# Moving 99 subtractions from GpSimd to VectorE in a hybrid Hyena and latent-attention layer

## The chip, the core and the metric

The kernel runs on one core of a Trainium2 chip, in one launch. The metric is the device time of one execution in microseconds (us). Five engines have queues of their own: TensorE (PE in the profile; PEld are its weight loads), VectorE (DVE), ScalarE (ACT), GpSimd (POOL) and SyncE (SP, which here only issues DMAs). An engine works its queue off in order; semaphores tie the queues to each other.

## The reference

```python
h = rms_norm(x, g_norm)                                   # x: (1, 1024, 1024) float32
proj = h @ w_in                                           # (1024, 1024) @ (1024, 5280)
hy_in, z_hy, c_q, c_kv, k_rope, z_attn, gate_hy, gate_attn = split(proj)
v_h, x1, x2 = split(short_conv(hy_in, w_short, b_short), 3)
k_spec = hyena_filter_spectra(...)                        # small MLP, two directions, rfft
zc = v_h
for o, gate in enumerate((x1, x2)):
    zc = gate * long_conv(zc, k_spec[:, o], hy_bias[o])   # FFT convolution, length 2048
u_hy = (zc * silu(z_hy)) @ w_hy_out
q, k, v = up-projections of rms_norm(c_q), rms_norm(c_kv); k_rope shared; rms_norm, rotary
u_attn = (attention(q, k, v) * silu(z_attn)) @ w_attn_out # 8 heads, 1024 x 1024 scores each
x + (sigmoid(gate_hy + b) * u_hy + sigmoid(gate_attn + b) * u_attn) @ w_out
```

Everything is float32.

## The kernel before

Every float32 product is made of three faster TensorE products: both operands are split into a high part (a cast on ScalarE, L133) and a low part (the operand less its high part, L134, a two-input subtraction), and high times high, low times high and high times low are summed in PSUM. `split` (L132) does that; its argument `eng` picks the engine of the subtraction, VectorE where none is given.

The stages follow one another on TensorE as follows. From 0 to 50 us `build_hT` loads and transposes x and makes `hh` and `hl`, the parts of the normalised input. From 50 to 250 us the filter's small MLP (`filter_mlp`, two sine layers of many VectorE steps), its tables and `filter_spectra` run: for each of 2 orders and 2 halves of the channels it forms, in four steps `tp`, the filter `kk` in both directions (PSUM times decay, L335), the sum `A` (L338, VectorE) and the difference `B` (L339, GpSimd). A butterfly on VectorE (`forward`) turns A and B into eight leaves, each split and multiplied with a table on TensorE (`leaf_fwd`, L128). From 250 to 650 us the four long convolutions (`conv`, `convs`) do the same forward and, leaf by leaf, back. From 650 to 775 us `qkv` and the rest of the projection follow, then attention, and from about 1020 us the tail with the output projections.

The big input projection is cut into 41 blocks of 128 columns and one of 32. `proj_block` (L538 on) makes one: for each of two halves of the rows it loads 128x512 weights `wr` (SP queue, 2 buffers), casts them to `wh` (ScalarE, 3 buffers), subtracts to `wl` (L134, on GpSimd, 3 buffers), and runs 24 products of 512 columns, among them `hh` times `wh`, `hl` times `wh` and `hh` times `wl` (L552). A half has to be consumed before its buffers take another. The last, small block (`proj_rope`, L565) does it in one piece. `branch_out` has a split of its own; its three calls with `mb == 1` are on GpSimd too, with the same tile names.

The queues do not have the order of the source: a planner places the instructions when the program is built, by durations of its own, and it may move any of them ahead of others that the data allow. Blocks of the projection are so mixed into the filter stage and the convolutions.

Of the kernel before, what the change touches and what calls it, by code (L numbers as in the profile page):

```python
# [10 lines left out]
F32 = mybir.dt.float32  # L11
# [3 lines left out]
ALU = mybir.AluOpType  # L15
# [77 lines left out]
class K:  # L93
# [219 lines left out]
    def filter_spectra(self, wk):  # L313
        nc, a = self.nc, self.a
        h2, w3h, w3l = self.h2, self.w3h, self.w3l
        kuh, kul = self.kuh, self.kul
        self.kd = {}
        for o in range(2):
            for hf in range(NHALF):
                A = wk.tile([P, 8, CW], F32, tag="A", name=self.nm("A"))  # L320
                B = wk.tile([P, 8, CW], F32, tag="B", name=self.nm("B"))
                cs = slice(hf * CW, (hf + 1) * CW)
                bia = wk.tile([1, CW], F32, tag="bia", bufs=2, name=self.nm("bia"))
                nc.sync.dma_start(out=bia, in_=a["hy_bias"][:, o, cs])
                for tp in range(4):
                    dec = wk.tile([P, 2, 2, CW], F32, tag="dec", bufs=2, name=self.nm("dec"))
                    nc.sync.dma_start(out=dec, in_=a["dec"][hf, tp].rearrange("p (d t c) -> p d t c", d=2, t=2))
                    kk = wk.tile([P, 2, 2, CW], F32, tag="kk", bufs=2, name=self.nm("kk"))
                    for d in range(2):
                        ps = self.pp.tile([P, 2, CW], F32, tag="cv", bufs=CVB, name=self.nm("pk"))  # L330
                        for i in range(2):
                            ts = slice((2 * tp + i) * P, (2 * tp + i + 1) * P)
                            nc.tensor.matmul(ps[:, i], lhsT=h2[d][:, ts], rhs=w3h[d][:, o, cs], start=True, stop=False)
                            nc.tensor.matmul(ps[:, i], lhsT=h2[d][:, ts], rhs=w3l[d][:, o, cs], start=False, stop=True)
                        nc.vector.tensor_tensor(out=kk[:, d], in0=ps, in1=dec[:, d], op=ALU.mult)  # L335
                    if tp == 0:
                        nc.vector.tensor_tensor(out=kk[0:1, 0, 0], in0=kk[0:1, 0, 0], in1=bia, op=ALU.add)
                    nc.vector.tensor_tensor(out=A[:, 2 * tp:2 * tp + 2], in0=kk[:, 0], in1=kk[:, 1], op=ALU.add)  # L338
                    nc.gpsimd.tensor_tensor(out=B[:, 2 * tp:2 * tp + 2], in0=kk[:, 0], in1=kk[:, 1], op=ALU.subtract)  # L339

                def take(k, ps):
                    if k == 0:
                        kt = wk.tile([P, 3, CW], F32, tag="kt0", bufs=1, name=self.nm("kt"))
                        nc.scalar.mul(out=kt[:, 0], in_=ps[:, 0], mul=2.0 ** -10)
                        nc.scalar.mul(out=kt[:, 1], in_=ps[:, 0], mul=2.0 ** -10)
                        nc.scalar.mul(out=kt[:, 2], in_=ps[:, 1], mul=2.0 ** -10)
                        nc.scalar.mul(out=kt[0:1, 1], in_=ps[0:1, 1], mul=2.0 ** -10)
                        nc.vector.memset(kt[0:1, 2], 0.0)
                        n = 3
                    else:  # L350
                        kt = wk.tile([P, 2, CW], F32, tag="kt", bufs=2, name=self.nm("kt"))
                        nc.scalar.mul(out=kt, in_=ps, mul=2.0 ** -10)
                        n = 2
                    kd = self.dp.tile([P, n, CW], F32, tag=f"kd{o}_{hf}_{k}", name=f"kd{o}_{hf}_{k + 8}")
                    nc.scalar.dma_start(out=kd, in_=kt)
                    self.kd[o, hf, k] = kd

                self.forward(A, B, kuh, kul, take)
# [178 lines left out]
    def proj_block(self, c0, m=P):  # L537

        nc, wp = self.nc, self.wp
        ps = [self.pp.tile([P, 512], F32, tag="mm", bufs=MMB, name=self.nm("pm")) for _ in range(2)]  # L540
        src = self.a["w_in"][0].rearrange("(d p) c -> p d c", p=P)
        for g in range(2):
            raw = wp.tile([P, 4, P], F32, tag="wr", bufs=2, name=self.nm("wr"))
            nc.sync.dma_start(out=raw[:, :, 0:m], in_=src[:, 4 * g:4 * g + 4, c0:c0 + m])
            wh = wp.tile([P, 4, P], F32R, tag="wh", bufs=3, name=self.nm("wh"))
            wl = wp.tile([P, 4, P], F32R, tag="wl", bufs=3, name=self.nm("wl"))
            self.split(raw[:, :, 0:m], wh[:, :, 0:m], wl[:, :, 0:m], self.nc.gpsimd)
            for i in range(4):
                d = 4 * g + i
                for (w, h, f) in ((wh, self.hh, 0), (wh, self.hl, 1), (wl, self.hh, 2)):  # L550
                    for c in range(2):
                        nc.tensor.matmul(ps[c][0:m], lhsT=w[:, i, 0:m], rhs=h[d][:, c * 512:(c + 1) * 512],  # L552
                                         start=(d == 0 and f == 0), stop=(d == 7 and f == 2))
        return ps

    def proj_rope(self, c0):

        nc, wp = self.nc, self.wp
        ps = [self.pp.tile([P, 512], F32, tag="mm", bufs=MMB, name=self.nm("pm")) for _ in range(2)]
        src = self.a["w_in"][0].rearrange("(d p) c -> p d c", p=P)  # L560
        raw = wp.tile([P, 8, 32], F32, tag="wr", bufs=2, name=self.nm("wr"))
        nc.sync.dma_start(out=raw, in_=src[:, :, c0:c0 + 32])
        w = wp.tile([P, 8, 64], F32R, tag="wh", bufs=3, name=self.nm("wh"))
        nc.scalar.copy(out=w[:, :, 0:32], in_=raw)
        nc.gpsimd.tensor_tensor(out=w[:, :, 32:64], in0=raw, in1=w[:, :, 0:32].bitcast(F32), op=ALU.subtract)  # L565
        for d in range(8):
            for f, h in enumerate((self.hh, self.hl)):
                for c in range(2):
                    nc.tensor.matmul(ps[c][0:64], lhsT=w[:, d], rhs=h[d][:, c * 512:(c + 1) * 512],
                                     start=(d == 0 and f == 0), stop=(d == 7 and f == 1))  # L570
        return ps
# [662 lines left out]
```

## Time and profile before

| | us |
|---|---|
| median of 3 runs (lowest, highest) | 1190.2 (1189.45, 1192.81) |
| the profiled execution | 1190.89 |
| its span, first to last instruction | 1189.1 |
| TensorE busy in the span | 1115.7 |
| VectorE busy | 899.3 |
| ScalarE busy | 584.0 |
| GpSimd busy | 282.9 |

Busy times are sums over the whole span; the stages have different limits, so the sections below go by stretches of it. TensorE's records overlap one another (a pair of products of 512 columns is recorded with 0.62 us around 736 us, and the next pair starts 0.45 us after it), so its idle time says more than its busy time. Of the 85 GpSimd subtractions called `wl`, 82 are the projection's and 3 those of `branch_out`.

### The profile page before, as it was taken

To read this page: it belongs to the slowest core of one execution; us is meant where nothing else is said; L and a number is where in the kernel's file an instruction comes from. 1 tells how busy PE (TensorE), PEld (TensorE's weight loads), DVE (VectorE), ACT (ScalarE), POOL (GpSimd) and SP (SyncE) were. 2 spreads that over 40 slices of the span, in tenths; PEclk is the share of its full clock that TensorE was granted. 3 is DMA by queue.
4 is the path that set the end of the run, shared out by engine and by line. 5 is a ranking of instruction groups with operands and counts; after the bars stand their busy time and mean duration, and the time that the engine had idled before them with its cause. 6 is when DMAs were issued, how large, how long until landed. Compare 5 with 4: busy or idle time off the path is not lost. (4 is left out here: it accounts for less than half of the span.)

```text
span 1189.1 us, 15596 instructions
## 1 busy us (share of the span) xinstructions
PE 1115.7 (94%) x5541; PEld 913.5 (77%) x5541; DVE 899.3 (76%) x1530; ACT 584.0 (49%) x1096; POOL 282.9 (24%) x217
## 2 busy tenths in 40 slices
PE   4989898999999999999999998999999999999996
PEld 3767777787888777787878887788887888777875
DVE  5889889977877986777764892188888898768873
ACT  5554455464424532434425742477777777422320
POOL 3333331333112121212111144500000000132253
PEclk7989999999999999999999999899999999999999
DMA  5334543553233424334227557620201010686245
GB/s 195 79 110 136 173 170 117 174 173 98 80 112 101 133 76 159 97 98 129 74 88 238 144 171 261 208 89 1 98 1 63 28 53 10 215 293 211 88 132 176
DMA packets 119221, 150.27 MB, mean 126 GB/s; under 512 B 8548, under 2 KB 82408, under 8 KB 119144
## 3 DMA queue, kind: packets, MB, share of 16 engines
q1 hardware_dynamic: 107832, 122.88, 33.6%
q10 hardware_dynamic: 11312, 26.42, 6.1%
q8 instruction: 43, 0.70, 0.3%
q14 instruction: 34, 0.28, 0.1%
HBM read 101.81 MB, written 47.45 MB: 126 GB/s over the span
## 5 line engine op out<-in xcount | busy, mean ns | idle before, releaser
L134 POOL TENSOR_TENSOR wl<-wr,wh 128x512 fp32r<-128x512 f32 x85 | 139.3, 1642 | 387.1 <-ACT wh L133 361.5
L552 PE MATMUL pm<-hh,wl 128*128 128x512 f32 x656 | 210.1, 396 | 3.2 <-POOL wl L134 3.2
L552 PE MATMUL pm<-hl,wh 128*128 128x512 f32 x656 | 212.5, 397 | 0.3 <-POOL hl L134 0.2
L552 PE MATMUL pm<-hh,wh 128*128 128x512 f32 x656 | 211.0, 397 | 1.7 <-ACT wh L133 1.7
L552 PEld LDWEIGHTS pm<-hh,wl 128*128 128x128 f32 x656 | 124.2, 190 | 29.6 <-POOL wl L134 4.1
L552 PEld LDWEIGHTS pm<-hh,wh 128*128 128x128 f32 x656 | 124.1, 190 | 28.1 <-ACT wh L133 2.5
L552 PEld LDWEIGHTS pm<-hl,wh 128*128 128x128 f32 x656 | 124.4, 190 | 27.0 <-DVE hl L134 1.0
L133 ACT CAST wh<-wr 128x512 fp32r<-128x512 f32 x98 | 60.3, 619 | 155.0 <-PE pm L552 108.4
L134 DVE TENSOR_TENSOR PTl<-pt,PTh 128x512 fp32r<-128x512 f32 x128 | 84.0, 683 | 14.0 <-ACT PTh L133 11.3
L133 ACT CAST PTh<-pt 128x512 fp32r<-128x512 f32 x128 | 72.8, 587 | 43.6 <-PE pt L886 41.0
L871 DVE TENSOR_REDUCE mx<-S 128x1 f32<-128x1024 f32 x64 | 77.8, 1218 | 10.5 <-PE S L122 10.0
L886 PE MATMUL pt<-ident,pr 128*128 128x128 f32 x512 | 75.1, 276 | 1.1 <-DVE PTl L134 0.5
L873 ACT ACTIVATE pr<-S,mx 128x1024 f32<-128x1024 f32 x64 | 71.7, 1120 | 5.4 <-DVE mx L871 5.1
L886 PEld LDWEIGHTS pt<-ident,pr 128*128 128x128 f32 x512 | 59.1, 140 | 15.5 <-ACT pr L873 2.9
L898 PE MATMUL pv<-PTh,vc 128*128 128x256 f32 x256 | 68.9, 297 | 0.0
L133 ACT CAST rh<-res 128x512 fp32r<-128x512 f32 x64 | 39.3, 617 | 59.3 <-DVE res L366 29.3
L899 PE MATMUL pv<-PTl,vc 128*128 128x256 f32 x256 | 67.8, 293 | 0.0
L458 DVE TENSOR_TENSOR t<-pu,kt 128x512 f32<-128x512 f32 x64 | 41.1, 682 | 34.8 <-PE pu L128 34.1
L967 DVE TENSOR_TENSOR gg<-gg,pmo 128x512 f32<-128x512 f32 x32 | 21.7, 679 | 46.9 <-DMA gT<-ob 44.1
L134 POOL TENSOR_TENSOR vc<-vr,vc 128x512 fp32r<-128x512 f32 x8 | 10.2, 1284 | 196.1 <-ACT vc L133 196.1
L118 PE MATMUL S<-kh,qh 96*128 96x512 f32 x128 | 53.0, 414 | 1.7 <-ACT pr L873 1.6
L121 PE MATMUL S<-kh,ql 96*128 96x512 f32 x128 | 52.5, 410 | 0.0
(289 smaller groups left out, 2580.8 us busy)
## 6 DMA issues: line engine op xcount, KB each, us to landing
wr<-in_w_in_dram SPq DMA_DIRECT2D x82, 256.0 KB, 3.0
wor<-in_w_out_dram SPq DMA_DIRECT2D x36, 256.0 KB, 5.1
dec<-in_dec_dram SPq DMA_DIRECT2D x16, 512.0 KB, 3.8
gT<-ob ACTq DMA_DIRECT2D x16, 512.0 KB, 3.6
gg<-gT SPq DMA_DIRECT2D x16, 512.0 KB, 4.7
kd<-kt ACTq DMA_DIRECT2D x28, 256.0 KB, 2.5
kt<-kd SPq DMA_DIRECT2D x28, 256.0 KB, 2.6
x<-in_x_dram SPq DMA_DIRECT2D x8, 512.0 KB, 6.2
```

The source lines that it names most:

```text
L118: m = nc.tensor.matmul(out, lhsT=lh, rhs=rh, start=start, stop=False)
L121: nc.tensor.matmul(out, lhsT=ll, rhs=rh, start=False, stop=False)
L133: self.nc.scalar.copy(out=hi, in_=x)
L134: (eng or self.nc.vector).tensor_tensor(out=lo, in0=x, in1=hi.bitcast(F32), op=ALU.subtract)
L458: tt = lambda o_, x, y, op: v.tensor_tensor(out=o_, in0=x, in1=y, op=op)
L552: nc.tensor.matmul(ps[c][0:m], lhsT=w[:, i, 0:m], rhs=h[d][:, c * 512:(c + 1) * 512], start=(d == 0 and f == 0), stop=(d == 7 and f == 2))
L871: nc.vector.tensor_reduce(out=mx, in_=ps, axis=AX.X, op=ALU.max, negate=True)
L873: nc.scalar.activation(out=pr, in_=ps, func=AF.Exp, bias=mx, accum_out=RS[h // 2][:, qb, h % 2:h % 2 + 1])
L886: nc.tensor.transpose(out=pt[:, i], in_=pr[:, kb * P:(kb + 1) * P], identity=self.ident)
L898: nc.tensor.matmul(pv, lhsT=V[h][:, kb], rhs=hi[:, kb], start=(kb == 0), stop=False)
L899: nc.tensor.matmul(pv, lhsT=V[h][:, kb], rhs=lo[:, kb], start=False, stop=(kb == 7))
L967: nc.vector.tensor_tensor(out=g[:, sl], in0=g[:, sl], in1=ps, op=ALU.mult)
```

## The change

Three subtractions go from GpSimd's queue to VectorE's: `B` in `filter_spectra` (16 instructions), the low part `wl` in `proj_block` (82) and the one in `proj_rope` (1). Operands, buffers, casts and DMAs are the same, and so is what is computed. GpSimd keeps its part in `build_hT` (`hl`, `zl`), in `qkv` (`k`), in `hyena_load` (`yl`), attention (`vc`), three splits of `branch_out` and the tail; between 50 and 650 us it is left with memsets alone.

```diff
@@ filter_spectra
                     nc.vector.tensor_tensor(out=A[:, 2 * tp:2 * tp + 2], in0=kk[:, 0], in1=kk[:, 1], op=ALU.add)
-                    nc.gpsimd.tensor_tensor(out=B[:, 2 * tp:2 * tp + 2], in0=kk[:, 0], in1=kk[:, 1], op=ALU.subtract)
+                    nc.vector.tensor_tensor(out=B[:, 2 * tp:2 * tp + 2], in0=kk[:, 0], in1=kk[:, 1], op=ALU.subtract)
@@ proj_block
-            self.split(raw[:, :, 0:m], wh[:, :, 0:m], wl[:, :, 0:m], self.nc.gpsimd)
+            self.split(raw[:, :, 0:m], wh[:, :, 0:m], wl[:, :, 0:m])
@@ proj_rope
-        nc.gpsimd.tensor_tensor(out=w[:, :, 32:64], in0=raw, in1=w[:, :, 0:32].bitcast(F32), op=ALU.subtract)
+        nc.vector.tensor_tensor(out=w[:, :, 32:64], in0=raw, in1=w[:, :, 0:32].bitcast(F32), op=ALU.subtract)
```

## Rows read from the trace of the kernel before

**Rows 1.** Busy time by stretch: us, then PE, PEld, DVE, ACT, POOL, clock, DMA, GB/s
```profile
50.00:250.00 200.00, 182.86 (x857) 146.78 (x856) 173.25 (x277) 107.25 (x206) 60.08 (x49) 0.97 0.46 147
250.00:650.00 400.00, 390.24 (x1781) 315.71 (x1780) 297.81 (x557) 167.41 (x329) 86.81 (x60) 1.00 0.39 116
650.00:775.00 125.00, 115.72 (x528) 95.85 (x526) 70.20 (x190) 60.81 (x113) 47.13 (x35) 0.97 0.61 192
```

**Rows 2.** Waits, 50 to 650 us: who waited for whom, us, times, longest
```profile
PE pu L128 <- ACT rh L133: 9.5, 7, 2.4
PE pm L552 <- POOL wl L134: 0.2, 1, 0.2
...
ACT wh L133 <- PE pm L552: 107.8, 28, 7.7
```

**Rows 3.** Durations by line and tile: minimum, median, maximum in ns
```profile
L134 DVE TENSOR_TENSOR rl<-res,rh x64: 669/679/1390, 104.7 to 593.0; 128x512 fp32r<-128x512 f32 x64
L335 DVE TENSOR_TENSOR kk<-pk,dec x32: 674/680/693, 86.1 to 218.5; 128x512 f32<-128x512 f32 x32
L338 DVE TENSOR_TENSOR A<-kk x16: 693/1477/1785, 88.2 to 219.4; 128x512 f32<-128x512 f32 x16
```

**Rows 4.** The group of projection subtractions on GpSimd, 50 to 250, then 250 to 650 us
```profile
L134 POOL TENSOR_TENSOR wl<-wr,wh 128x512 fp32r<-128x512 f32 x19 | 33.3, 1754 | 76.1 <-ACT wh L133 69.6 <-PE pu L128 5.8 <-PE pm L552 0.7
...
L134 POOL TENSOR_TENSOR wl<-wr,wh 128x512 fp32r<-128x512 f32 x51 | 85.1, 1670 | 302.3 <-ACT wh L133 288.0 <-PE pm L552 10.2 <-DMA wr<-in_w_in_dram 4.2
```

**Rows 5.** In order of time, one step of the filter: VectorE, then GpSimd
```profile
97.77 1.78 DVE L338 TENSOR_TENSOR A<-kk 128x512 f32<-128x512 f32 x1
...
97.60 1.41 POOL L339 TENSOR_TENSOR B<-kk 128x512 f32<-128x512 f32 x1 [1.83 <-DVE kk L335]
```

**Rows 6.** In order of time, VectorE: lengthened instructions beside GpSimd reads
```profile
62.70 1.07 DVE L245 SCALAR_TENSOR_TENSOR sx<-sk,sx 128x512 f32<-128x512 f32 x1
64.03 0.68 DVE L245 SCALAR_TENSOR_TENSOR sx<-sk,sx 128x512 f32<-128x512 f32 x1
67.17 1.78 DVE L245 SCALAR_TENSOR_TENSOR sx<-sk,sx 128x512 f32<-128x512 f32 x1
65.90 1.35 DVE L134 TENSOR_TENSOR kul<-kur,kuh 128x1152 fp32r<-128x1152 f32 x1
68.88 2.41 DVE L134 TENSOR_TENSOR kul<-kur,kuh 128x1152 fp32r<-128x1152 f32 x1
237.70 0.74 DVE L367 SCALAR_TENSOR_TENSOR res<-w,w 128x256 f32<-128x256 f32 x2
240.34 1.67 DVE L367 SCALAR_TENSOR_TENSOR res<-w,w 128x256 f32<-128x256 f32 x2
253.19 1.90 DVE L584 SCALAR_TENSOR_TENSOR acc<-sraw,cols,acc 128x1024 f32<-128x1024 f32 x1 [0.34 <-ACT acc L583]
642.56 1.21 DVE L138 SCALAR_TENSOR_TENSOR cl<-cr,cols,ch 128x256 fp32r<-128x256 f32 x1 [0.23 <-ACT ch L137]
```

**Rows 7.** In order of time around 740 us: TensorE, then GpSimd
```profile
739.94 0.73 PE L552 MATMUL pm<-hh,wh 128*128 128x512 f32 x2 [1.70 <-ACT wh L133]
744.13 1.22 PE L552 MATMUL pm<-hh,wl 128*128 128x512 f32 x2 [2.99 <-POOL wl L134]
738.17 4.68 POOL L134 TENSOR_TENSOR yl<-yr,yh 128x1024 fp32r<-128x1024 f32 x2 [9.97 <-ACT yh L133]
742.81 1.26 POOL L134 TENSOR_TENSOR wl<-wr,wh 128x512 fp32r<-128x512 f32 x1
```

**Rows 8.** Busy time by stretch as in rows 1, at two places
```profile
745.00:750.00 5.00, 5.00 (x13) 3.83 (x13) 0.00 (x0) 3.16 (x6) 5.00 (x4) 0.51 0.84 264
70.00:78.00 8.00, 5.94 (x19) 5.08 (x20) 7.74 (x8) 2.48 (x4) 2.00 (x4) 0.57 0.35 94
```

**Rows 9.** In order of time, TensorE: its waits in the filter stage
```profile
72.06 0.58 PE L333 MATMUL pk<-w3h,h 128*128 128x256 f32 x1 [3.69 <-DVE h L291]
104.56 0.41 PE L128 MATMUL pu<-rh,kuh 128*128 128x256 f32 x1 [2.36 <-ACT rh L133]
```

## The prediction

> **What bounds the kernel now.** I read the busy time by stretch first, then what TensorE waits for, then durations of the moved operations and of what runs beside them. TensorE is the bound: it is idle for 17.1 us between 50 and 250 us (200 less 182.9), for 9.8 us between 250 and 650 and for 9.3 us between 650 and 775 [rows 1]. Work taken off any other engine can only give back what lies in those 36 us, or what a low TensorE clock costs behind an idle time. VectorE is second: busy for 173.3 us of 200 in the filter stage, with 26.8 idle, and for 297.8 of 400 in the convolutions [rows 1]. TensorE's waits in these 600 us are for the ends of VectorE's chains (a cast of `res`, 9.5 us); for the moved `wl` it waits 0.2 us [rows 2]. So the change matters in two ways: by what it does to VectorE's chains, and by the one place after 650 us where `wl` was late.
>
> **What one moved instruction costs on VectorE.** The same operation, shape and type is there already: `rl<-res,rh`, 0.68 us in the median [rows 3]. I take 0.68 us for each of `wl` and `B`, and 0.4 us for the half-size one of `proj_rope` (an estimate by size).
>
> **What it gives back on VectorE.** An instruction there with both inputs in SBUF that meets a GpSimd subtraction waits for the rest of it. `A` and `B` are released together and read the same `kk`: `A` takes 1.48 us in the median and 0.69 when alone, while `kk<-pk,dec`, whose one input is in PSUM, never leaves 0.67 to 0.69 [rows 3]; one such meeting is shown, `B` from 97.60 and `A` for 1.78 us [rows 5]. I summed, over all VectorE instructions that overlap a GpSimd read which the change moves, their duration less that of the same shape alone. From 50 to 250 us that is 25.3 us in 28 instructions, the first of them the sine step at 62.70 (1.07 us for 0.68), the last within the pair at 240.34 (1.67 us, where the pair before took 0.74); from 250 to 650 us it is 26.6 us in 32 instructions, from 253.19 to 642.56 [rows 6].
>
> The Trainium skill (SBUF — State Buffer, section Who interferes with whom) has this as a rule: a VectorE instruction with two SBUF inputs and a GpSimd one that reads SBUF lock each other out, and whoever issues first keeps the port for its whole length. The trace agrees, with 1.48 us for `A` and 0.68 for `kk`.
>
> **50 to 250 us.** On VectorE come 19 `wl` [rows 4] and 16 `B`, as many as there are `A` [rows 3]: 35 times 0.68 is 23.8 us; 25.3 us go. The load falls by 1.5 us, in effect not at all. What can change is the length of the chains for which TensorE stands. In the MLP it waits 3.69 us for `h` at 72.06 [rows 9]; three stalls are in VectorE's queue ahead of it, 0.39 and 1.10 us in sine steps and 1.06 us in `kul` [rows 6], 2.55 us in all, and three `wl` (2.0 us) take their place if the planner leaves them there. That is -0.5 to -2.6 us, and the clock is granted at 0.57 from 70 to 78 us after that wait [rows 8], so a shorter wait may also save part of 3.4 us (8 times 0.43). In each of the four filter steps some 3.1 us of stalls on `A` go (4 times 0.78) against four `B` (2.7 us); about four `wl` come (2.7 us) against the quarter of what other stalls are left, 2.6 us (25.3 less 2.55 less 12.5, over 4). Net -0.3 us each, -1.2 for four, more if the planner sets `B`, which only the last four leaves need, behind the sums. TensorE's wait at 104.56, 2.36 us, shows that the end of such a step is bare [rows 9]. I take -3 us for this stage. The bounds are -17, all of its idle time, and +10, if the `wl` of the four steps stand bare (10.8 us, less the 1.2).
>
> **250 to 650 us.** 51 `wl` [rows 4] and the one of `proj_rope` are 35.1 us more, 26.6 go: VectorE from 297.8 to about 306 of 400 us. TensorE has 9.8 us of idle time here, and 0.2 us of it (from 50 us on) was for `wl` [rows 1, 2]. I take 0, with -6 and +6 as bounds: more than half of the idle time would have to go for the one, and the 8.5 us of extra load would have to stand nearly bare for the other. What hides that load is the half block of products that TensorE has in hand when the next half's parts are made: 24 of them at about 0.22 us (390.2 us over 1781 [rows 1]) are 5.3 us, against 0.62 us more of latency where one other VectorE instruction is ahead. Without that cover each `wl` would cost its 0.68 us, 35 us in all.
>
> **650 to 775 us.** At 744.13 TensorE waits 2.99 us for a `wl` that was ready to start at 739.94, when its `wh` was there, but stood behind two `yl` of 4.68 us in GpSimd's queue until 742.81 [rows 7]. On VectorE, which does nothing between 745 and 750 us [rows 8], it would be there at 740.6, before TensorE asks. That is -3.0 us. The clock is at 0.51 from 745 to 750 [rows 8], 2.4 us of TensorE time lost; but the wait of 1.70 us for `wh` just before stays [rows 7], so I count 1.5 of the 2.4. Together -4.5 us, with -5.4 and 0 (if the load of `wr`, which the earlier release of its buffer starts sooner, lands no sooner) as bounds. `yl` itself starts its second pair 1.3 us earlier, which nothing needs.
>
> **0 to 50 us and the end.** The 4 `wl` left there (85 less 19, 51 and 11, three of the last staying on GpSimd) are 2.7 us on VectorE against stalls of the same kind; I take 0, plus or minus 2.7. From 775 us on nothing is changed.
>
> **The sum.** -3, 0, -4.5 and 0 are -7.5 us. The profiled execution took 1190.9 us, so 1183.4; it stands 0.7 us above the median of the runs, 1190.2. I forecast 1183 us. The forecast's own range, 1174 to 1187, takes half of the idle time of the filter stage at one end and the late `wl` alone at the other.
>
> **Rivals.** First: nothing to measure, 1187 to 1193, 1190 at its middle. TensorE is the bound, the weights are early by half a block, and VectorE's load is the same; after the late `wl` TensorE waits as long for the next `wr`. For it: 0.2 us of waits on `wl` in 600 us [rows 2]. Against it: 3 us stand bare at 744.13 [rows 7].
>
> Second, slower: VectorE's queue stands. Moved `wl` are instructions that wait, for `wh` on ScalarE, which itself waits 28 times, 107.8 us in all and up to 7.7 us at once, until TensorE has freed a buffer [rows 2]. On GpSimd only other `wl` and `B` stood behind such a wait; on VectorE the butterfly of the filter and of the convolutions does, and TensorE waits for that. It decides where the planner sets a `wl` ahead of a chain's step and the wait is longer than TensorE's 5.3 us in hand; 7.7 less 5.3 is 2.4 us a time. With some two to five such places, and the chains later by a `wl` each at as many, on top of a gain that fails, it is 5 to 15 us: 1195 to 1205. Against it: ScalarE has the same order and the same wait, and TensorE is still idle for only 9.8 us of 400 [rows 1].
>
> Third, slower too: the stalls don't go, so that the 23.8 us are simply added to the 173.3 us in 200. Then the four filter steps get 2.7 us longer by `B` and as much by `wl`, 21.6 us on top of the forecast, and 1205 is the time. The Trainium skill (Perfetto Trace Analysis, section Optimizing Scalar/DVE Operations) speaks for it: where VectorE is saturated, giving work to GpSimd may help, and this change does the reverse; the same passage adds that the shared port can make such a move useless. In this trace the stalls lie beside GpSimd's reads and nowhere else in `kk` or `A`, so it gets little.
>
> That some GpSimd reads remain is no rival between 50 and 650 us: `wl`, `B` and `proj_rope`'s are all that it reads there.
>
> **Chances.** Forecast 0.55, better than its range 0.04, first rival 0.22, second 0.15, third 0.04. Faster by over 0.3% (below 1186.6; 0.3% is about what a measurement of this kernel tells from no change) is 0.58, within it 0.23, slower 0.19. The range that should hold 8 in 10 goes from 1173 to 1201: it leaves out the better case, the third rival and the upper part of the second, some 0.13.
>
> **What would show it.** `A` at 0.69 us and `rl` without its 1.39 us maximum; VectorE's busy time within 10 us of 899 in spite of 99 more instructions; no wait of TensorE for `wl` near 744, with the clock less low behind it; the wait for `h` at 72 shorter. Wrong it is if VectorE shows waits for ScalarE's `wh` of several us with TensorE idle behind them, or if the idle time of TensorE between 50 and 650 us, 27 us now, grows.

## The result and the profile after

The changed kernel takes 1177.96 us in the median of 4 runs (1174.73 to 1179.6), the kernel before beside it 1190.51. The ratio is 0.9896, interval [0.9872, 0.9920]: 12.4 us less. The forecast was 1183, 7 us less, and its range held the time. The sum was short by 5 us, and by stages it was further off than that.

Busy time by stretch, columns as in [rows 1], three stages after:

```profile
50.00:250.00 200.00, 180.44 (x840) 145.48 (x840) 178.58 (x327) 111.61 (x214) 0.93 (x14) 0.94 0.47 152
250.00:650.00 400.00, 397.43 (x1838) 327.45 (x1837) 298.83 (x613) 171.08 (x338) 0.53 (x8) 1.00 0.39 119
650.00:775.00 125.00, 120.10 (x576) 100.32 (x575) 78.49 (x194) 62.37 (x116) 36.29 (x27) 0.99 0.56 184
```

Set against [rows 1]: TensorE's idle time goes from 9.8 to 2.6 us in 250 to 650 and from 9.3 to 4.9 in 650 to 775, but from 17.1 up to 19.6 in the filter stage, at a lower granted clock there (0.94 for 0.97). By TensorE's idle time the gain sits where the forecast had 0, and where it had -3 there is none. The same instructions do not fall into the same stretch in both kernels (the planner has laid the queues out anew), so the stretches say where to look and the runs below give the prices.

Durations after (minimum, median, maximum in ns), to be read beside [rows 3]: the stalls are gone.

```profile
L338 DVE TENSOR_TENSOR A<-kk x16: 669/682/692, 83.5 to 204.7; 128x512 f32<-128x512 f32 x16
L134 DVE TENSOR_TENSOR rl<-res,rh x64: 669/680/694, 96.2 to 578.9; 128x512 fp32r<-128x512 f32 x64
```

TensorE's two costliest waits after in 50 to 250 us (total, times, longest), its first two there in order of time, and the last product `pf` of the MLP ahead of them, first before, then after:

```profile
PE pk L333 <- DVE h L291: 6.5, 1, 6.5
PE pu L128 <- ACT rh L133: 4.8, 1, 4.8
...
67.81 0.58 PE L333 MATMUL pk<-w3h,h 128*128 128x256 f32 x1 [6.45 <-DVE h L291]
71.97 1.97 PE L596 MATMUL ptt<-ident,acc 128*128 128x128 f32 x8 [2.09 <-DVE acc L585]
...
59.80 0.50 PE L122 MATMUL pf<-h1l,w2h 128*128 128x512 f32 x1
58.11 0.50 PE L122 MATMUL pf<-h1l,w2h 128*128 128x512 f32 x1
```

`h` is there at 67.81, where TensorE had it at 72.06 before [rows 9]: 4.3 us earlier. Of these, 1.7 us are already there at the last `pf`; the chain from there to `h` takes 9.7 us instead of 12.3, shorter by the three stalls of 2.55 us. Yet TensorE's wait for `h` has grown from 3.69 to 6.45 us. It came to the wait earlier, because it had fewer projection products to do meanwhile. VectorE's queue tells why: two `wl` stand behind that chain.

```profile
70.64 1.28 DVE L585 SCALAR_TENSOR_TENSOR acc<-sraw,cols,acc 128x1024 f32<-128x1024 f32 x1
71.84 0.68 DVE L134 TENSOR_TENSOR wl<-wr,wh 128x512 fp32r<-128x512 f32 x1
72.55 1.41 DVE L291 TENSOR_TENSOR h<-sx,h 64x512 fp32r<-64x512 f32 x2
73.99 0.69 DVE L134 TENSOR_TENSOR wl<-wr,wh 128x512 fp32r<-128x512 f32 x1
```

### The profile page after: what moved, and what is told of

The parts are those of the page before. It is cut to its first block, busy times and chain, and to the rows that moved or that the text cites. A ratio compares the mean times of both kernels' runs of the same rounds, so it can differ in the third digit from the quotient of the medians.

```text
span 1174.9 us, 15580 instructions
## 1 busy us (share of the span) xinstructions
PE 1111.1 (95%) x5541; PEld 916.1 (78%) x5541; DVE 902.8 (77%) x1629; ACT 585.0 (50%) x1096; POOL 121.2 (10%) x118
## 4 chain that ended last, share of the span: by engine, by line
PE 72%; DVE 12%; DMA 7%; ACT 5%; issue 2%; POOL 1%; SPq 0%; POOLq 0%; DVEq 0%; ACTq 0%
PE pm L552 32%; PE pu L128 6%; PE pt L886 5%; PE pi L128 4%; PE S L118 2%; PE S L121 2%; PE S L122 2%; PE pmo L118 2%; PE pv L898 2%; PE pmo L121 2%; PE pmo L122 2%; PE pv L899 2%; PE po L121 2%; PE po L118 2%; PE po L122 2%
## 5 line engine op out<-in xcount | busy, mean ns | idle before, releaser
L552 PE MATMUL pm<-hl,wh 128*128 128x512 f32 x656 | 210.1, 395 | 0.5 <-POOL hl L134 0.4
L552 PEld LDWEIGHTS pm<-hl,wh 128*128 128x128 f32 x656 | 123.9, 190 | 26.6 <-POOL hl L134 1.2
L134 DVE TENSOR_TENSOR wl<-wr,wh 128x512 fp32r<-128x512 f32 x95 | 71.1, 751 | 43.4 <-ACT wh L133 43.0
L873 ACT ACTIVATE pr<-S,mx 128x1024 f32<-128x1024 f32 x64 | 71.7, 1121 | 5.7 <-DVE mx L871 5.1
L898 PEld LDWEIGHTS pv<-PTh,vc 128*128 128x128 f32 x256 | 48.6, 190 | 4.4 <-DVE at L909 1.6
L799 POOL TENSOR_TENSOR k<-k,ry 128x512 f32<-128x512 f32 x8 | 11.6, 1452 | 380.8 <-DVE rv L146 377.4
```

Source lines behind the costliest of these rows:

```text
L134: (eng or self.nc.vector).tensor_tensor(out=lo, in0=x, in1=hi.bitcast(F32), op=ALU.subtract)
L873: nc.scalar.activation(out=pr, in_=ps, func=AF.Exp, bias=mx, accum_out=RS[h // 2][:, qb, h % 2:h % 2 + 1])
L898: nc.tensor.matmul(pv, lhsT=V[h][:, kb], rhs=hi[:, kb], start=(kb == 0), stop=False)
```

## The experiments

Two causes were open from the start, since the change moves work and makes the planner order everything anew: 1837 of TensorE's 5541 products stand at another place of its queue. So most runs hold one of the two fixed. A chain of edges without waits, added when the program is built, puts each engine's instructions into a recorded order; only the moved subtractions take a place that the planner picks. In the traces of e1 to e7 and e9 to e11 every other instruction of an engine stands in the recorded order. Each time is compared with the kernel before on the same chip (1188.0, 1189.3 and 1188.5 us in the three groups e1 to e4, e5 to e8, e9 to e12). Microseconds of gain or loss are the ratio less 1, times 1189.

| run | order of | subtractions on VectorE | us | ratio, interval | gain or loss |
|---|---|---|---|---|---|
| changed kernel | planner | all | 1177.96 | 0.9896 [0.9872, 0.9920] | -12.4 |
| e1 | before | all | 1182.96 | 0.9955 [0.9936, 0.9975] | -5.4 |
| e2 | changed | none | 1192.79 | 1.0036 [1.0020, 1.0051] | +4.3 |
| e3 | changed | all, GpSimd also reads | 1202.23 | 1.0117 [1.0093, 1.0141] | +13.9 |
| e4 | before | B | 1187.71 | 0.9994 [0.9980, 1.0008] | -0.7 |
| e5 | before | wl to 230 us | 1200.53 | 1.0092 [1.0077, 1.0107] | +10.9 |
| e6 | before | wl from 650 us | 1184.05 | 0.9955 [0.9938, 0.9972] | -5.4 |
| e7 | before | B, wl from 230 us | 1174.12 | 0.9877 [0.9857, 0.9897] | -14.6 |
| e8 | planner | as e7 | 1166.23 | 0.9800 [0.9781, 0.9818] | -23.8 |
| e9 | before | wl 230 to 650 us | 1182.94 | 0.9948 [0.9931, 0.9965] | -6.2 |
| e10 | changed | all, GpSimd also reads hh | 1201.35 | 1.0107 [1.0086, 1.0127] | +12.7 |
| e11 | changed | all, GpSimd also writes | 1175.48 | 0.9893 [0.9872, 0.9914] | -12.7 |
| e12 | planner | as e8, and yl | 1165.80 | 0.9812 [0.9790, 0.9835] | -22.4 |

### Engines or order: e1, e2

```diff
     with tile.TileContext(nc) as tc:
-        hyena_mla_kernel(tc, aps, out)
+        hyena_mla_kernel(tc, aps, out); in_order(tc)
...
+def in_order(tc):
...
+    traced = {i.name: i for i in tc.nc.cur_bb.bb.instructions}
+    no = mybir.DependencyInfo(mybir.DependencyClass.NoSync, mybir.DependencyReason.DATA)
+    for steps in json.loads(zlib.decompress(base64.b85decode(ORDER))):
+        names = [f"I-{n}" for n in itertools.accumulate(steps)]
+        names = [n for n in names if n in traced]
+        for a, b in zip(names, names[1:]):
+            tc.add_manual_dep(traced[b], a, no, reason="order")
```

`ORDER` is the packed list of the recorded order. e1 is the changed kernel with the order of the kernel before, e2 the kernel before with the order of the changed one.

> The changed kernel with every instruction of TensorE, ScalarE, VectorE, SyncE and GpSimd that both kernels have chained in the order of the kernel before; only the moved subtractions take a free place. Two theories of the 12.5 us. Engines: the gain is that GpSimd's reads no longer stall VectorE and its results no longer come late; then this kernel keeps most of it, 1177 to 1182 us, and TensorE's idle time in 250 to 650 us falls from 9.8 to under 4 us. Order: the planner has laid the program out anew on four engines (1572 of some 9600 lines of TensorE's order differ) and the gain is that order; then this kernel stays at 1187 to 1193 us.

> The kernel before, subtractions on GpSimd as they were, with every other instruction chained in the order of the changed kernel. Engines: the time stays at 1186 to 1195 us and VectorE's instructions beside GpSimd's reads are stalled for some 50 us between 50 and 650 us, as before. Order: 1176 to 1181 us in spite of those stalls.

Neither theory holds alone. e1 lies between its two ranges; e2 lies in its first, the one of the engines. The moved work in the old order gives 5.4 of the 12.4 us, and the new order on the old engines costs 4.3. The order is worth something only together with the move, some 7 us of the 12.4. Why the move alone gives no more stands in e1's waits, 50 to 250 us:

```profile
PE pm L552 <- DVE wl L134: 19.1, 3, 11.3
```

For `wl` TensorE had waited 0.2 us in 600 us [rows 2]. By TensorE's idle time the new order saves more in the filter stage (23.9 us idle in e1, 19.6 in the changed kernel) than in the convolutions (4.0 and 2.6).

### Part by part in the old order: e4, e5, e6, e9

e4 is the first pair of lines of the diff alone. The others choose the engine of `wl` by the running number of the block:

```diff
-            self.split(raw[:, :, 0:m], wh[:, :, 0:m], wl[:, :, 0:m], self.nc.gpsimd)
+            self.split(raw[:, :, 0:m], wh[:, :, 0:m], wl[:, :, 0:m], None if (lambda n: n < 770)(self.nid) else self.nc.gpsimd)
```

with `n < 770` for the first 22 (e5), `n >= 1486` for the last 8 (e6), and between the two for 53 (e9, `proj_rope`'s among them). The expectation of e6 speaks of 11; three of these are `branch_out`'s, which the edit leaves on GpSimd: of 85 `wl` there, 77 are left in e6's trace.

> The kernel before in its own order, with only the 16 subtractions B on VectorE (16 x 0.68 us added, the stall of A beside them gone). My forecast's term for it is a part of the filter stage's -3 us: 1187 to 1191 us. If the whole gain came from the filter stage's end moving earlier (it ends 16 us earlier in the changed kernel): 1178 to 1184 us.

> The kernel before in its own order; on VectorE are only the 22 subtractions wl that GpSimd did in the first 230 us, everything else stays on GpSimd. Queue theory: VectorE works in order, so a wl behind the filter's own instructions comes later than GpSimd's, and TensorE waits for it, as it did in e1 (19.1 us in three places, 11.3 at 72 us); then this kernel is slower, 1193 to 1200 us. Contention theory alone (each read that leaves GpSimd frees VectorE by its stall): 1184 to 1187 us. No effect: 1187 to 1191 us.

> The kernel before in its own order; on VectorE are only the last 11 subtractions wl, from 650 us on. My forecast's third term stands or falls with it: 4.5 us less (the 3.0 us wait for wl at 744 us and 1.5 us of clock), so 1183 to 1186 us, and no wait for wl near 744 us. If the next operand is as late (gg, ob, or the input weights): 1187 to 1190 us.

> The kernel before in its own order; on VectorE are only the 53 subtractions wl from 230 to 650 us. My forecast gave this stage 0 (bounds -6 and +6): 1183 to 1195 us. If the parts add up (e7 is 15.2 us faster than the kernel before, of which B has about 1 and the last stage 5.2), the convolution stage has 9 us: 1178 to 1182 us.

`B` alone gives nothing that can be measured. The `wl` of the first 230 us on VectorE cost 10.9 us, half a us more than the queue theory's range, and the waits are those of e1 again: 19.1 us for `wl` in three places, of which 11.2 are one. That one in order of time in e5: TensorE, VectorE's queue ahead of it, and ScalarE; and, last, GpSimd and TensorE at this place in the kernel before:

```profile
60.57 0.63 PE L552 MATMUL pm<-hl,wh 128*128 128x512 f32 x2
72.44 1.22 PE L552 MATMUL pm<-hh,wl 128*128 128x512 f32 x2 [11.24 <-DVE wl L134]
...
79.21 0.28 PE L333 MATMUL pk<-w3h,h 128*128 128x256 f32 x1
...
66.93 1.40 DVE L291 TENSOR_TENSOR h<-sx,h 64x512 fp32r<-64x512 f32 x2
68.36 0.69 DVE L245 SCALAR_TENSOR_TENSOR sx<-sk,sx 128x512 f32<-128x512 f32 x1
68.97 1.28 DVE L584 SCALAR_TENSOR_TENSOR acc<-sraw,cols,acc 128x1024 f32<-128x1024 f32 x1
70.17 0.42 DVE L247 TENSOR_SCALAR sx<-sx 128x512 f32<-128x512 f32 x1
70.50 1.27 DVE L585 SCALAR_TENSOR_TENSOR acc<-sraw,cols,acc 128x1024 f32<-128x1024 f32 x1
71.70 1.28 DVE L134 TENSOR_TENSOR wl<-wr,wh 128x512 fp32r<-128x512 f32 x2
...
59.32 0.62 ACT L133 CAST wh<-wr 128x512 fp32r<-128x512 f32 x1
63.73 0.60 ACT L133 CAST wh<-wr 128x512 fp32r<-128x512 f32 x1
...
61.86 1.36 POOL L134 TENSOR_TENSOR wl<-wr,wh 128x512 fp32r<-128x512 f32 x1 [13.92 <-ACT wh L133]
67.98 0.39 PE L552 MATMUL pm<-hh,wh 128*128 128x512 f32 x1
```

The operands of the two `wl` were there at 59.9 and 64.3 us; VectorE, busy without a gap with the MLP, a table and a short convolution, came to them at 71.70. `h`, the chain's end, was done by 68.3 us; TensorE got to it at 79.21, because the projection products stand ahead of it in its queue. In the kernel before, GpSimd made the first of them at 61.86, as soon as its `wh` was there, and TensorE had products to do until 68.37 while the MLP ran on VectorE. That is the cover which the move took away. The two `wl` stand behind the chain because the planner put them there; a place ahead of the chain's steps was not tried (an estimate from their duration: it would hold the chain up by 0.7 us for each).

e6 gives 5.4 us, and its mechanism is the forecast's. Columns as in [rows 1], 740 to 745 us before, then 740 to 750 in e6, to be read beside [rows 8]:

```profile
740.00:745.00 5.00, 2.01 (x6) 1.39 (x7) 0.00 (x0) 1.76 (x2) 5.00 (x4) 0.81 0.78 211
...
740.00:745.00 5.00, 4.71 (x20) 3.30 (x18) 2.43 (x1) 3.25 (x5) 5.00 (x3) 1.00 0.97 324
745.00:750.00 5.00, 4.83 (x20) 3.67 (x20) 0.09 (x1) 0.62 (x1) 2.48 (x2) 1.00 0.82 272
```

TensorE is idle for 0.3 us of the first five where it had been for 3.0, and the clock, 0.51 from 745 on before, is granted whole.

e9 gives 6.2 us in the stage that had 0 in the forecast; its 1182.9 us are at the edge of the first range and 1 us above the second. Busy time of 250 to 650 us in e9, then TensorE's waits there: in the kernel before, and in e9.

```profile
250.00:650.00 400.00, 395.98 (x1816) 324.52 (x1815) 305.63 (x616) 173.22 (x339) 0.53 (x8) 1.00 0.39 120
...
PE pu L128 <- ACT rh L133: 3.2, 3, 2.2
PE ptt L596 <- DVE acc L585: 1.8, 2, 1.4
PE pty L700 <- DVE Y L458: 1.8, 1, 1.8
PE pty L700 <- DVE Y L459: 1.6, 2, 0.9
...
PE pq L118 <- ACT ch L137: 1.8, 1, 1.8
PE pty L700 <- DVE Y L459: 0.7, 2, 0.4
PE pu L128 <- ACT rh L133: 0.3, 1, 0.3
PE pty L700 <- DVE Y L458: 0.3, 1, 0.3
PE ptt L596 <- DVE acc L585: 0.2, 1, 0.2
```

VectorE's load has risen to 305.6 us, as forecast, and all the same the waits for the ends of its chains (`rh`, `acc`, `Y`) go from 8.4 us to 1.5. Of VectorE's own waits in this stretch, 12.5 us are now for `wh`, 8 times and up to 3.3 us; nothing on TensorE stands idle behind them.

The four parts add up to -1.4 us, e1 has -5.4; without the filter's `wl` they add up to -12.3, and e7 has -14.6. Each figure is uncertain by 2 us or so, so the parts act almost, but perhaps not quite, independently of each other.

### The stalls by themselves: e3, e10, e11

All three keep the changed kernel's engines and its order, and give GpSimd something to do beside each moved subtraction (98 of the 99) that nobody reads (the lines are shortened; the memset of e11 is twice as wide):

```diff
 e3
+            ...; again(self, wh[:, :, 0:m].bitcast(F32), wh[:, :, 0:m].bitcast(F32), "w")
+def again(k, x, y, t):
+    j = k.wp.tile(list(x.shape), F32, tag="junk" + t, bufs=1, name=f"junk_{k.n_again}")
+    ...k.nc.gpsimd.tensor_tensor(out=j, in0=x, in1=y, op=ALU.subtract)...
 e10: the same with both operands k.hh[0][:, 0:512], ordered behind wh (or A) by an edge
 e11
-    m = k.nc.gpsimd.tensor_tensor(out=j, in0=x, in1=x, op=ALU.subtract)
+    m = k.nc.gpsimd.memset(j, 0.0)
```

> The changed kernel in its own order on every engine, and GpSimd also does beside each moved subtraction one of the same size whose result nobody reads (wh minus wh, A minus A). VectorE is stalled by the reads again, but no matmul waits for GpSimd. If the stalls of VectorE were what cost the time: back to 1186 to 1191 us. If it was that GpSimd handed wl and B over late: 1177 to 1180 us, with the stalls there and nothing lost by them. If it was the order: 1177 to 1180 us too, and e2 tells these two apart.

> The changed kernel in its own order on every engine; beside each moved subtraction GpSimd does one of the same size that reads hh twice, a tile that lies there unchanged, and nobody reads its result. Unlike in e3 it holds no wh back. If e3's 24 us over the changed kernel were the stalls of VectorE: 1196 to 1203 us. If much of it was ScalarE's wait for the wh that GpSimd still read (14.1 us in four places in e3): 1182 to 1194 us.

> As e10, with a memset of 128x1024 in the place of each of GpSimd's unread subtractions: the same waits and a similar time on GpSimd (a memset of 64x1024 took 0.95 us), but it reads no SBUF. If it is GpSimd's reads that stall VectorE: 1177 to 1181 us and VectorE's instructions at their own durations. If any work of GpSimd on SBUF does it: 1188 to 1203 us.

The reads cost 25 to 26 us over the changed kernel, whether they hold a `wh` back (e3) or not (e10); the writes cost nothing. e10 came inside its first range, e3 above all of its ranges (VectorE now has the moved work and the stalls as well), e11 1.5 us below its first. What GpSimd did in e10 and in e11, and three groups of VectorE from 250 to 650 us (busy us and mean ns), first in e11, then in e10:

```profile
L1242 POOL MEMSET junk<- x98: 950/955/968, 26.0 to 739.3; 128x1024 f32 x98
L458 DVE TENSOR_TENSOR t<-pu,kt 128x512 f32<-128x512 f32 x62 | 39.8, 682 | 35.1 <-PE pu L128 34.4
L134 DVE TENSOR_TENSOR wl<-wr,wh 128x512 fp32r<-128x512 f32 x52 | 35.4, 682 | 14.4 <-ACT wh L133 14.0
L458 DVE TENSOR_TENSOR p<-t,t 128x256 f32<-128x256 f32 x64 | 24.1, 417 | 0.3
...
L1243 POOL TENSOR_TENSOR junk<-hh x98: 1035/1357/8127, 25.4 to 762.0; 128x512 f32<-128x512 f32 x98
L458 DVE TENSOR_TENSOR t<-pu,kt 128x512 f32<-128x512 f32 x64 | 41.1, 682 | 29.6 <-PE pu L128 28.9
L134 DVE TENSOR_TENSOR wl<-wr,wh 128x512 fp32r<-128x512 f32 x51 | 39.0, 767 | 12.8 <-ACT wh L133 12.6
L458 DVE TENSOR_TENSOR p<-t,t 128x256 f32<-128x256 f32 x64 | 27.5, 469 | 0.3
```

`t`, with one operand in PSUM, keeps its 682 ns; `wl` and `p`, with both in SBUF, are longer by 85 and 52 in the mean. Over the span VectorE is busy for 901.1 us in e11 and for 944.5 in e10: 43 us of stalls, and 26 us of time. With this order and these engines more than half of a stalled microsecond is lost.

The Trainium skill (SBUF — State Buffer, section Who interferes with whom) says that a VectorE instruction with two SBUF inputs contends with a GpSimd one that reads SBUF, and not with one that only writes it. e10 and e11 agree, with 1201.35 and 1175.48 us.

### What the parts point to: e7, e8, e12

e7 leaves the first 22 `wl` on GpSimd (`n >= 770` in the edit of e5) and has `B` on VectorE, in the old order; e8 is the same without the chain of order; e12 adds `yl` and the three splits of `branch_out` that were on GpSimd:

```diff
-            self.split(r, wh, wl, nc.gpsimd if self.mb == 1 else nc.vector)
+            self.split(r, wh, wl, nc.vector)
-            self.split(y, self.yh[i], self.yl[i], nc.gpsimd)
+            self.split(y, self.yh[i], self.yl[i])
```

> The kernel before in its own order; on VectorE are B and the wl from 230 us on, while the first 22 wl stay on GpSimd. If the parts add up as e1 and e4 have them (B about -4 us by the working of the filter stage in its profile, the convolution stage -6.5, the last stage -6 to -7.5): 1171 to 1176 us, faster than the changed kernel. If e1's late gains were only the filter's loss handed back (work that was held up earlier finding free room later): 1181 to 1186 us.

> The same engines as e7, with the order left to the planner, as in the changed kernel. If the planner's order is what fits the moved work to VectorE's queue (the changed kernel is 5 us faster than e1): 1168 to 1174 us. If its new order brings the front's loss with it whatever the engines (+6 to +8 us by 60 us in e2 and e3): 1176 to 1182 us.

> e8 with the four subtractions yl and the last wl ahead of the attention on VectorE too. In e8 TensorE waits 3.7 us for a wl that GpSimd hands over behind its yl near 738 us, while VectorE is busy 0.7 us of 720 to 740 us. If that wait is the limit there: 2 to 4 us under e8, 1162 to 1165 us. If the transfers are (DMA share 0.91 from 730 to 740 us): 1165 to 1168 us.

e7 came at 1174.1, inside its first range, and e8 at 1166.2, below both of its ranges; by the ratios e8 is some 11 us under the changed kernel. Busy time by stretch in e8, 50 to 250 us and 250 to 650:

```profile
50.00:250.00 200.00, 191.15 (x918) 155.92 (x917) 178.56 (x302) 114.87 (x216) 38.79 (x34) 0.99 0.48 155
250.00:650.00 400.00, 397.69 (x1832) 326.79 (x1830) 300.36 (x615) 169.75 (x335) 0.40 (x6) 1.00 0.39 121
```

The filter stage is where it differs from the changed kernel: TensorE is idle for 8.9 us instead of 19.6, at 0.99 of the clock instead of 0.94, although GpSimd is still busy there for 38.8 us, 37.9 of them with `wl`. The convolutions are as in the changed kernel, 2.3 us idle. e12 is the same as e8 within the intervals: the wait of 3.7 us for `wl` has gone down to 0.2 and the one for `gg` has grown from 1.7 to 6.8 us. By its own terms its 1165.8 us fall to the second of its two expectations; that the transfers are the limit there is not shown by it.

## Why the prediction was right, and where it was not

**The cost of a moved instruction, and the stalls.** Right. `A` is at 0.68 us and `rl` never above 0.694; VectorE's busy time is 902.8 us, 3.5 above before, with 99 more instructions. In e9 its load from 250 to 650 us is 305.6, where the working had about 306. The third rival, stalls that don't go, is out.

**650 to 775 us, -4.5.** Right in size and by its mechanism: e6 gives 5.4 us (3.3 to 7.4 by its interval), through the wait at 744 and the clock behind it.

**250 to 650 us, 0.** This term was mis-sized: e9 gives 6.2 us (4.2 to 8.2), at the edge of the bound of -6. The step that failed is the balance itself: 35.1 us on, 26.6 us off, hence nothing. The two are not worth the same. The stalls lay inside the chains for whose ends TensorE waits (`rh`, `Y`, `acc`); the added `wl` lie in time in which VectorE has 102 us idle out of 400 [rows 1], and no matmul of e9 waits for them there. The stage had the cover that the prediction named; it should have followed that the stalls come off and the load costs nothing.

**50 to 250 us, -3.** Wrong, and this is the step that failed worst: e4 and e5 together give some +10 in the old order, and in the changed kernel TensorE is idle there for 2.4 us more than before. The working set stalls of 25.3 us against an added 23.8 in a queue that has 27 us idle, and took the small difference for the answer. In the old order the `wl` of the first 230 us cost 10.9 us (e5). That is near the +10 that stood as a bound, but by luck: the bound was for the four filter steps, and 11.2 of the 19.1 us of waits lie in the MLP. `B`, four times 2.7 us against 3.1, gave nothing that can be measured (e4), as worked out. The three stalls ahead of `h` went as the working had it, 2.55 us; the wait for `h` grew all the same: the working followed VectorE's chain alone and missed that the projection products were TensorE's work during that chain. The sentence that 5.3 us of products in hand hide a late `wl` was made for the convolutions, where it holds; in the MLP the first of the two `wl` waits in VectorE's queue for nearly 12 us (in e5 from 59.9, when its `wh` is there, to 71.7).

**0 to 50 us, 0.** Inside its bounds of 2.7, but perhaps not nothing: the last `pf` starts at 58.0 to 58.4 us in the four profiles with these four `wl` on VectorE and no added reads (changed kernel, e1, e5, e11), and at 58.9 to 61.0 in the eight with them on GpSimd.

**The second rival.** Its engine and its price were there (19.1 us of TensorE's waits in e1, 10.9 us of time in e5, forecast 5 to 15), but the longest wait is in the MLP and not at a butterfly, and the direction is reversed. It had the `wl` wait for `wh` and hold up the chain. That happens, up to 3.3 us in e9 and 5.7 in the changed kernel, and costs nothing that these runs show. What costs is the chain holding up the `wl`. It did not decide the sign: in e1, which has these waits, the other stages outweigh them (-5.4 us), and in the changed kernel's order TensorE waits 0.2 us for `wl` in the filter stage.

**What the prediction left out.** That the planner lays the whole program out anew. The working took each `wl` to stand where it stood. Between e1 and the changed kernel only the order differs, and that is 7 us; the same order with the old engines is 4.3 us slower than the kernel before. That the range held the time is in good part luck. The forecast of -7 came within 5 us of -12.4 because three terms of which it had none at its size nearly cancel: +10.9 (the filter's `wl`), -6.2 (the convolutions) and -7 (the order) are -2.3 together, where the sum had -3 and 0.

What stays open: how much of the 7 us of the new order is saved in the filter stage and how much in the convolutions (the idle times of e1 and the changed kernel point to the filter stage, but their stretches do not hold the same instructions); whether the surplus of 2 to 4 us over the parts' sum is real; and whether a `wl` set ahead of the MLP's steps would have spared the 10.9 us.

## What to carry to other kernels

A balance of busy time (so much on, so much off) does not price a move between engines. Ask for each stage whether what goes stood inside a chain that the bound engine waits for, and whether what comes has idle time to stand in; here the same `wl` were worth -6 us in one stage and +11 in another, and the two fastest kernels here (e8 and e12, 1166 us) leave the latter where they were.

Work that covers a long chain on one engine is better not fed from behind that chain. Where the bound engine has filler to do during a chain, look at who makes the filler's operands; if the move puts them into the chain's queue behind its steps, the cover is gone, and the wait shows up as the filler's, not the chain's.

Where a planner orders the program, a change of an engine is two changes. Fixing the order with a chain of edges separates them, and here gave parts that nearly add up.

## What had not been expected of the hardware

A GpSimd subtraction beside a busy VectorE was held up as well: in e10 98 equal ones took 1.04 us at least, 1.36 in the median and up to 8.1, while the memsets of e11 stayed between 0.950 and 0.968 us beside the same instructions. The longest one and, of VectorE's instructions that ran without a gap from 404.80 to 412.5 us at their usual lengths, one that falls inside it:

```profile
405.33 8.13 POOL L1243 TENSOR_TENSOR junk<-hh 128x512 f32<-128x512 f32 x1 [6.45 <-ACT wh L133]
...
408.21 1.21 DVE L366 TENSOR_TENSOR w<-U 128x1024 f32<-128x1024 f32 x1
```

In e10 the price goes both ways; the memsets of e11, which read nothing, neither pay it nor cost it.

The clock behind a wait of TensorE did not follow the length of the wait. Columns as in [rows 1], 72 to 78 us, behind the wait of 3.69 us in the kernel before, the one of 3.72 us in e4 and the one of 11.24 us in e5:

```profile
72.00:78.00 6.00, 5.94 (x19) 5.08 (x20) 5.77 (x7) 1.87 (x4) 1.93 (x3) 0.54 0.26 68
...
72.00:78.00 6.00, 6.00 (x28) 5.25 (x29) 5.78 (x7) 1.97 (x4) 1.75 (x3) 0.75 0.19 51
...
72.00:78.00 6.00, 5.56 (x16) 4.48 (x17) 1.67 (x3) 0.62 (x1) 0.06 (x2) 0.63 0.35 93
```

In all three the clock is at the lower of its two levels (0.50) from 72 to 74 us and whole again (1.00) from 78 to 80. Of the three means the one behind the longest wait stands in the middle.
